# Attention with two value passes, denominators summed by accumulating DMAs, scores two key tiles ahead of the products, and each head's preparation in 28 slots

## The chip, the cores and the metric

The kernel runs on one core of one Trainium2 chip. The metric is the device time of one execution in microseconds (us). The engines of the core are called as the profile calls them: PE (TensorE, the matrix engine; PEld is its weight load), DVE (VectorE), ACT (ScalarE), POOL (GpSimd) and SP (SyncE, which here only issues DMAs). PE multiplies into PSUM, a memory of eight banks of 128 rows by 512 numbers; everything else lies in SBUF or in DRAM.

## The reference

One layer of a hybrid network over 1024 latent tokens and 256 context tokens, with model width 1024. A recurrent branch and an attention branch are gated, added and projected; then a mixture of 16 experts follows. The change touches the attention branch alone, which is

```python
def attend(q_nope, q_rope, k_nope, k_rope, v):
    s = (jnp.einsum('bqhd,bkhd->bhqk', q_nope, k_nope)
         + jnp.einsum('bqhr,bkr->bhqk', q_rope, k_rope)).astype(jnp.float32) * ATTN_SCALE
    prob = jax.nn.softmax(s, axis=-1).astype(v.dtype)
    return jnp.einsum('bhqk,bkhd->bqhd', prob, v)
```

with 8 heads, 1024 queries, 1280 keys (context and latent together), 96 numbers of a query or key (64 and 32) and 64 of a value. Before it the kernel computes the recurrent branch's output projection, after it the attention's output projection, the merge and the experts.

## The kernel before

Matmuls of full precision are split: a float32 array x is kept as a high part xh in the type fp32r and a low part xl = x - xh, made by a cast on ACT and a subtraction on DVE (`split`, lines 94 and 95), and a product takes three fp32r passes, hh, hl and lh (`mm3`, lines 98 to 100). A matmul on plain float32 operands needs no split.

The stage loops over 8 heads (h) and within a head over 10 key tiles (kt) of 128 keys. Keys lie on the partitions and the 1024 queries on the free axis, in two halves (n). For a key tile, `scores` multiplies kh, kl with qh, ql into the PSUM tile s (three buffers), ACT takes the exponential of it into pr, and pr is split into ph and pl. The products then multiply ph, pl with the values into the two PSUM tiles po, one for each half. A value tile vh, vl has 128 columns: 64 are the head's values, the other 64 are ones in vh and zeros in vl, so that 64 rows of po hold the numerators and the other 64 the denominators. Two of the ten tiles (FULL = (0, 5)) go unsplit: pr times a float32 value tile vf. Scores run one key tile ahead of the products.

While a head runs, the next one is prepared (`head_ops`): transposes of its raw keys and queries into the PSUM tiles qkt and their splits kl, ql; 32 matmuls of 320 keys by 128 queries into the PSUM tile pm, each reduced on DVE to its row maximum mx; and two steps `fin` that transpose the maxima (mr) and let ACT write them, negated, into row 0 of qh. All of these share the tag "pm", three PSUM banks. The 40 slots of a head are four for each key tile: before the scores of either half, and before the products of either half. The 39 steps are spread over 34 slots, the second `fin` is in slot 36.

At the head's end `finish` copies numerators (num) and denominators (den) out of po with four ACT copies; po has no second pair of buffers, so the next head's first products wait for them. After each second head `norm_step` takes a reciprocal of den on DVE, multiplies on POOL and splits the result into ath, atl, in eight pieces.

PE's instructions stand in the order in which the code issues them (a manual schedule). On DVE, ACT, POOL and SP a scheduler decides the order when the program is built; it is fixed then, and each engine works through its own order without overtaking. DMAs are issued by SP unless the code says `nc.gpsimd`.

Of the kernel before, what the change touches and what calls it, by code (L numbers as in the profile page):

```python
# [27 lines left out]
P = 128  # L28
# [32 lines left out]
def layer_kernel(ctx: ExitStack, tc: tile.TileContext, I, rope_tab, out, dbg=None):  # L61
# [64 lines left out]
    mod_d = dram.tile([4, D], F32, name="mod_d")  # L126

# [630 lines left out]
    vt = {}  # L758
    for e in range(2):
        for nm, val in (("h", 1.0), ("l", 0.0)):  # L760
            v = p5.tile([P, NKT, P], F32R, name=f"v{nm}{e}")
            vt[nm, e] = v
            o = slice(VH, P) if e == 0 else slice(0, VH)
            nc.vector.tensor_scalar(v[:, :, o], ident[:, None, 0:VH].to_broadcast([P, NKT, VH]), 0.0, val,
                                    op0=OP.mult, op1=OP.add)
    QT, dn, PR = {}, {}, {}
    FULL = (0, 5)
    vf = []
    for e in range(2):
        v = p5.tile([P, len(FULL), P], F32, name=f"vf{e}")  # L770
        nc.gpsimd.memset(v[:, :, slice(VH, P) if e == 0 else slice(0, VH)], 1.0)
        vf.append(v)

# [5 lines left out]
    def load_head(h):  # L779
        kraw = p5.tile([P, 1024], F32, name="kraw", bufs=2)[:, 0:NKT * KA].rearrange("p (t d) -> p t d", d=KA)  # L780
        nc.sync.dma_start(kraw, k_d[h])
        qraw = p5.tile([P, 896], F32, name="qraw", bufs=2)[:, 0:NT * KA].rearrange("p (t d) -> p t d", d=KA)
        nc.sync.dma_start(qraw, q_d[h])
        vraw = p5.tile([P, NKT, VH], F32, name="vraw", bufs=2)
        nc.sync.dma_start(vraw, v_d[h])
        PR[h] = (qraw, kraw, vraw)

    def head_ops(h):
# [6 lines left out]
        mx = p5.tile([P, 64], F32, name="mx", bufs=2)[:, 0:4 * NT].rearrange("p (g t) -> p g t", t=NT)  # L795
        QT[h] = (qh, ql, kh, kl, mx)
        o = slice(0, VH) if e == 0 else slice(VH, P)
# [15 lines left out]
        def pmx(t, g):  # L813
            def f():
                pm = pm1("pm")
                nc.tensor.matmul(pm[:, 0:320], qh[:, t * P:(t + 1) * P], kh[:, g * 320:(g + 1) * 320],  # L816
                                 start=True, stop=True)
                nc.vector.tensor_reduce(mx[:, g, t:t + 1], pm[:, 0:320], axis=AX.X, op=OP.max)  # L818
            return f

        def fin(n):
            def f():
                tt = slice(4 * n, 4 * n + 4)
                nc.vector.tensor_tensor(mx[:, 0:2, tt], mx[:, 0:2, tt], mx[:, 2:4, tt], OP.max)
                nc.vector.tensor_tensor(mx[:, 0, tt], mx[:, 0, tt], mx[:, 1, tt], OP.max)
# [10 lines left out]
        seq += [pmx(t, g) for g in (1, 2, 3) for t in range(4)] + [pmx(t, 0) for t in range(4, 8)]  # L836
        seq += [fin(0)] + [pmx(t, g) for g in (1, 2, 3) for t in range(4, 8)]
# [6 lines left out]
    load_head(1)  # L844
# [13 lines left out]
    for b in range(KD):  # L858
# [11 lines left out]
        for _ in range(len(pre) if b == KD - 1 else max(0, 7 * (b - 1))):  # L870
            if pre:
                pre.pop(0)()
    mrow = p4.tile([16, P], F32, name="mrow2")
# [21 lines left out]
    with pool("p5a") as p5a:  # L895
        def scores(h, kt, side=None):
            qh, ql, kh, kl, _ = QT[h]
            ks = slice(kt * P, (kt + 1) * P)
            pr = p5a.tile([P, SEQ], F32, name="pr", bufs=3)
# [7 lines left out]
            if kt in FULL:  # L907
                return pr, None
            ph = p5a.tile([P, SEQ], F32R, name="ph", bufs=2)
            pl = p5a.tile([P, SEQ], F32R, name="pl", bufs=2)  # L910
            split(ph, pl, pr)
            return ph, pl

        def finish(h, po):
            e, j = h % 2, h // 2
            if e == 0:
                dn["n"] = p5a.tile([P, SEQ], F32, name="num", bufs=1)
                dn["d"] = p5a.tile([P, SEQ], F32, name="den", bufs=1)
            num, den = dn["n"], dn["d"]
# [448 lines left out]
```

## Time and profile before

| | |
|---|---|
| time, median of 3 runs | 1768.45 us (1767.8 to 1769.65) |
| the profiled execution's own time | 1771.81 us |
| its span, first to last instruction | 1769.8 us, so 2.0 us lie around it |
| busy share of the span: PE, PEld, DVE, ACT, POOL | 95%, 77%, 74%, 57%, 15% |
| the attention stage, first scores to last products | from 688.2 to 988.3 us |

Busy time of PE is not PE at its peak: a matmul's record lasts longer than the distance to the next one that follows it without a gap. So the text counts PE's work by the distance between starts. A row of a timeline or of a chain gives the start, the duration, the engine, the line and the operation with its output and inputs; "x2" means that two are merged into the row. A wait row says who waited for whom, the sum, how often, and the longest.

### The profile page before, as it was taken

The numbers are of one execution on the slowest core, as the hardware profiler recorded it, in microseconds if no ns is written. First come the engines' busy times: TensorE is split into PE (matmuls) and PEld (weight loads), VectorE is DVE, ScalarE is ACT, GpSimd is POOL, SyncE is SP. The second block draws the span as 40 slices with busy tenths as digits, with TensorE's granted clock in tenths as the row PEclk, the third lists the DMA queues.
The fourth block names the chain that finished last, engine by engine and source line by source line (L and its number), as shares of the span: only waits on it lengthen the run. The fifth ranks groups of instructions, "written<-read, shape, count | busy, mean of one in ns | idle before, by whom it ended". The sixth has DMA issues, their size and how long they took to land.

```text
span 1769.8 us, 20838 instructions
## 1 busy us (share of the span) xinstructions
PE 1687.1 (95%) x7823; PEld 1356.9 (77%) x7823; DVE 1313.4 (74%) x1607; ACT 1014.9 (57%) x1105; POOL 264.5 (15%) x196
## 2 busy tenths in 40 slices
PE   8999999999999999999999999939999999999996
PEld 3788887888887877777777678827888888888885
DVE  4755456788886454787877657587999999989996
ACT  2533324876788313667776532316777777777773
POOL 1123331211221100111210100020121111112101
PEclk9999999999999999999999999969999999999999
DMA  8264444435443934000000355667999999999981
GB/s 328 100 181 101 108 121 140 131 126 167 155 144 117 318 136 152 28 28 28 29 1 1 138 199 213 234 261 286 379 395 391 403 399 381 399 402 380 389 309 24
DMA packets 174179, 363.72 MB, mean 206 GB/s; under 512 B 40160, under 2 KB 90744, under 8 KB 174080
## 3 DMA queue, kind: packets, MB, share of 16 engines
q1 hardware_dynamic: 168896, 343.54, 53.6%
q0 software_dynamic: 5184, 18.88, 4.0%
q8 instruction: 61, 1.00, 0.2%
q14 instruction: 38, 0.31, 0.0%
HBM read 314.84 MB, written 47.54 MB: 205 GB/s over the span
## 4 chain that ended last, share of the span: by engine, by line
PE 71%; DVE 11%; ACT 6%; issue 4%; DMA 4%; POOL 3%; SPq 0%; POOLq 0%; DVEq 0%; ACTq 0%
PE w_e_gate L99 3%; PE w_e_gate L100 3%; PE w_e_gate L98 3%; PE w_e_down L99 3%; PE w_e_down L100 3%; PE w_e_down L98 3%; PE w_e_up L99 3%; PE w_e_up L98 3%; PE w_e_up L100 3%; PE z L99 2%; PE z L98 2%; PE z L100 2%; PE pm L816 2%; POOL st L143 2%; PE s L98 2%
## 5 line engine op out<-in xcount | busy, mean ns | idle before, releaser
L95 DVE TENSOR_TENSOR el<-ma,eh 128x2048 fp32r<-128x2048 f32 x114 | 258.2, 2286 | 22.2 <-PE w_e_down L99 10.8
L94 ACT CAST eh<-ma 128x2048 fp32r<-128x2048 f32 x114 | 217.9, 1917 | 73.7 <-PE w_e_up L100 28.7
L95 DVE TENSOR_TENSOR el<-me,eh 128x2048 fp32r<-128x2048 f32 x78 | 176.9, 2287 | 16.6 <-ACT eh L94 6.0
L94 ACT CAST eh<-me 128x2048 fp32r<-128x2048 f32 x78 | 149.0, 1916 | 47.4 <-PE w_e_gate L100 17.3
L906 ACT ACTIVATE pr<-s 128x512 f32<-128x512 f32 x160 | 95.8, 599 | 77.2 <-PE s L100 75.8
L818 DVE TENSOR_REDUCE mx<-pm 128x1 f32<-128x320 f32 x256 | 114.4, 483 | 22.8 <-PE pm L816 20.6
L99 PE MATMUL z<-xl,wh 128*128 128x512 f32 x320 | 125.2, 392 | 1.9 <-DVE xl L280 1.9
L98 PE MATMUL z<-xh,wh 128*128 128x512 f32 x320 | 125.2, 393 | 1.0 <-DVE xh L279 0.8
L100 PE MATMUL z<-xh,wl 128*128 128x512 f32 x320 | 125.0, 391 | 1.2 <-POOL wl L326 1.2
L1312 POOL DMA_INDIRECT out_dram<-y,icol x16 | 52.3, 3268 | 469.9 <-DVE y L1311 469.9
L94 ACT CAST wh<-wr 128x1024 fp32r<-128x1024 f32 (+1 forms) x53 | 52.0, 980 | 116.1 <-PE z L99 55.0
L95 DVE TENSOR_TENSOR pl<-pr,ph 128x1024 fp32r<-128x1024 f32 x64 | 81.0, 1265 | 31.4 <-ACT ph L94 24.7
L99 PE MATMUL w_e_up<-el,xgh 128*128 128x512 f32 x256 | 100.7, 394 | 0.6 <-DVE el L95 0.6
L98 PE MATMUL w_e_gate<-eh,xgh 128*128 128x512 f32 x256 | 101.1, 395 | 0.2 <-ACT xgh L94 0.2
L99 PE MATMUL w_e_gate<-el,xgh 128*128 128x512 f32 x256 | 101.2, 395 | 0.0
L100 PE MATMUL w_e_gate<-eh,xgl 128*128 128x512 f32 x256 | 100.1, 391 | 0.8 <-DVE xgl L95 0.8
L98 PE MATMUL w_e_down<-eh,hdh 128*128 128x512 f32 x256 | 99.7, 389 | 1.1 <-ACT hdh L94 1.1
L98 PE MATMUL w_e_up<-eh,xgh 128*128 128x512 f32 x256 | 100.7, 393 | 0.0
L99 PE MATMUL w_e_down<-el,hdh 128*128 128x512 f32 x256 | 100.6, 393 | 0.0
L100 PE MATMUL w_e_down<-eh,hdl 128*128 128x512 f32 x256 | 99.9, 390 | 0.5 <-DVE hdl L95 0.5
L100 PE MATMUL w_e_up<-eh,xgl 128*128 128x512 f32 x256 | 99.8, 390 | 0.0
L816 PE MATMUL pm<-kh,qh 97*128 97x320 f32 x256 | 86.6, 353 | 7.0 <-DVE kl L95 4.1
(349 smaller groups left out, 4368.7 us busy)
## 6 DMA issues: line engine op xcount, KB each, us to landing
ma<-in_w_e_down_dram SPq DMA_DIRECT2D x40, 1024.0 KB, 9.4
ma<-in_w_e_up_dram SPq DMA_DIRECT2D x38, 1024.0 KB, 8.0
ma<-in_w_e_gate_dram SPq DMA_DIRECT2D x36, 1024.0 KB, 7.2
me<-in_w_e_gate_dram SPq DMA_DIRECT2D x28, 1024.0 KB, 7.0
me<-in_w_e_up_dram SPq DMA_DIRECT2D x26, 1024.0 KB, 8.2
me<-in_w_e_down_dram SPq DMA_DIRECT2D x24, 1024.0 KB, 9.8
wr<-in_w_in_dram SPq DMA_DIRECT2D x32, 512.0 KB, 4.5
wr<-in_w_ada_dram SPq DMA_DIRECT2D x32, 512.0 KB, 4.2
```

The source lines that it names most:

```text
L94: nc.scalar.copy(h, src)
L95: nc.vector.tensor_tensor(l, src, h.bitcast(F32), OP.subtract)
L98: nc.tensor.matmul(o, lh, rh, start=start, stop=False)
L99: nc.tensor.matmul(o, lh, rl, start=False, stop=False)
L100: nc.tensor.matmul(o, ll, rh, start=False, stop=stop)
L143: nc.gpsimd.tensor_tensor(ap, ap, h, OP.pow)
L816: nc.tensor.matmul(pm[:, 0:320], qh[:, t * P:(t + 1) * P], kh[:, g * 320:(g + 1) * 320], start=True, stop=True)
L818: nc.vector.tensor_reduce(mx[:, g, t:t + 1], pm[:, 0:320], axis=AX.X, op=OP.max)
L906: nc.scalar.activation(pr[:, sl], sp_, AF.Exp)
L1312: nc.gpsimd.indirect_dma_start(out=out_rows, out_offset=bass.IndirectOffsetOnAxis(ap=icol[:, e:e + 1], axis=0), in_=y, in_offset=None, com ...
```

## The change

Values. A value tile v now holds the high parts in 64 columns and the low parts in the other 64, so a key tile needs two passes, ph and pl, and po holds ph·vh + pl·vh in one half of its rows and ph·vl + pl·vl in the other; `finish` copies one half on ACT and adds the other on DVE. Only one tile is unsplit, FULL = (5,).

Denominators. The ones are gone. The exponentials of key tiles 0 and 1 stay in two tiles "sum"; those of tiles 2 to 9 are added to them by DMAs that POOL issues with an accumulate, even tiles to one, odd to the other, and a last one adds the two. In the next head's key tile 4, `denominators` multiplies the sum with a column of ones (float32, into dp), and four DMAs of SP bring the row through DRAM into 128 partitions for the reciprocal and back, repeated over 64 partitions. The last head sums on PE instead (`last_sums`).

Order. Scores run two key tiles ahead. The row maxima use 24 matmuls, 16 of 512 keys and 8 of 256. The 31 steps of a head's preparation are spread over 28 slots, the second `fin` is in slot 31. kraw, qraw and vraw have one buffer each in place of two, and num takes a buffer of the weight ring "wr".

```diff
-    vt = {}
-    for e in range(2):
-        for nm, val in (("h", 1.0), ("l", 0.0)):
-            v = p5.tile([P, NKT, P], F32R, name=f"v{nm}{e}")
...
+    vt = [p5.tile([P, NKT, P], F32R, name=f"v{e}") for e in range(2)]
-    FULL = (0, 5)
+    FULL = (5,)
...
         def tv():
-            nc.scalar.copy(vt["h", e][:, :, o], vraw)
-            nc.gpsimd.tensor_tensor(vt["l", e][:, :, o], vraw, vt["h", e][:, :, o].bitcast(F32), OP.subtract)
+            nc.scalar.copy(vt[e][:, :, o], vraw)
+            nc.gpsimd.tensor_tensor(vt[e][:, :, o2], vraw, vt[e][:, :, o].bitcast(F32), OP.subtract)
...
-                nc.tensor.matmul(pm[:, 0:320], qh[:, t * P:(t + 1) * P], kh[:, g * 320:(g + 1) * 320],
-                                 start=True, stop=True)
-                nc.vector.tensor_reduce(mx[:, g, t:t + 1], pm[:, 0:320], axis=AX.X, op=OP.max)
+                ks = slice(g * 512, min(TOK, (g + 1) * 512))
+                n = ks.stop - ks.start
+                nc.tensor.matmul(pm[:, 0:n], qh[:, t * P:(t + 1) * P], kh[:, ks], start=True, stop=True)
+                nc.vector.tensor_reduce(mx[:, g, t:t + 1], pm[:, 0:n], axis=AX.X, op=OP.max)
...
-            slots[i * 34 // len(seq)].append(f)
-        slots[36].append(fin(1))
+            slots[i * 28 // len(seq)].append(f)
+        slots[31].append(fin(1))
...
+            if kt < 2:
+                sums[h, kt] = pr
+            elif h < HEADS - 1 or kt < NKT - 2:
+                nc.gpsimd.dma_start(out=sums[h, kt % 2], in_=pr, accum_op=OP.add)
...
-                nc.scalar.copy(den[no, sl], po[n][do, :])
-                nc.scalar.copy(num[no, sl], po[n][no, :])
+                nc.scalar.copy(num[no, sl], po[n][do, :])
+                nc.vector.tensor_tensor(num[no, sl], num[no, sl], po[n][no, :], OP.add)
...
+            if h < HEADS - 1:
+                nc.gpsimd.dma_start(out=sums[h, 0], in_=sums.pop((h, 1)), accum_op=OP.add)
+        def denominators(h, num, rec):
+            acc = sums.pop((h, 0))
+            no = lanes(h)[0]
+            row = rec[no.start:no.start + 1, :]
+            for n in range(2):
+                sl = slice(n * 512, (n + 1) * 512)
+                dp = pm1("dp")
+                nc.tensor.matmul(dp[0:1, :], ones, acc[:, sl], start=True, stop=True)
+                nc.scalar.copy(row[:, sl], dp[0:1, :])
+            nc.sync.dma_start(den_d[h:h + 1, :], row)
+            rs = p5a.tile([P, 8], F32, name="rs", bufs=2)
+            nc.sync.dma_start(rs, den_d[h].rearrange("(p j) -> p j", j=8))
+            nc.vector.reciprocal(rs, rs)
+            nc.sync.dma_start(rec_d[h].rearrange("(p j) -> p j", j=8), rs)
+            row = rec_d[h]
+            nc.sync.dma_start(rec[no, :], bass.AP(tensor=row.tensor, offset=row.offset, ap=[[0, VH], [1, SEQ]]))
...
-                if i + 1 < len(steps):
-                    nxt = scores(*steps[i + 1], side)
+                if i + 2 < len(steps):
+                    ahead2.append(scores(*steps[i + 2], side))
...
+                for t in (ph, pl):
+                    side(2 + (t is pl))
+                    for n in range(2):
+                        sl = slice(n * 512, (n + 1) * 512)
+                        if pl is None and t is ph:
+                            nc.tensor.matmul(po[n], vf[h % 2][:, FULL.index(kt)], ph[:, sl], start=kt == 0, stop=kt == NKT - 1)
+                        elif pl is not None:
+                            nc.tensor.matmul(po[n], vt[h % 2][:, kt], t[:, sl], start=kt == 0 and t is ph,
+                                             stop=kt == NKT - 1 and t is pl)
+                if kt == 4 and h:
+                    denominators(h - 1, dn["n"], dn["r"])
```

Outside this stage the order on every engine is what it was, but for a few loads on SP. On DVE, in a head with no normalisation in it, from the last split of transposed queries (ql) on, before:

```order
L95 TENSOR_TENSOR ql<-qkt,qh 97x512
L818 TENSOR_REDUCE mx<-pm 128x1 x2
L95 TENSOR_TENSOR pl<-pr,ph 128x1024
L818 TENSOR_REDUCE mx<-pm 128x1 x4
L95 TENSOR_TENSOR pl<-pr,ph 128x1024
L818 TENSOR_REDUCE mx<-pm 128x1 x5
```

and now, in the same place:

```order
L95 TENSOR_TENSOR ql<-qkt,qh 97x512
L818 TENSOR_REDUCE mx<-pm 128x1
L95 TENSOR_TENSOR pl<-pr,ph 128x1024
L818 TENSOR_REDUCE mx<-pm 128x1 x3
L95 TENSOR_TENSOR pl<-pr,ph 128x1024
L818 TENSOR_REDUCE mx<-pm 128x1 x6
```

The splits pl now stand between groups of one, three and six reductions, and these reductions are of 512 columns in the first two groups and the first two rows of the third. On ACT, at the end of the third head (h = 2, where the first pair of heads is normalised in the changed kernel), before:

```order
L829 ACTIVATE qh<-mr 1x512
L906 ACTIVATE pr<-s 128x512 x2
L923 COPY den<-po 64x512
L924 COPY num<-po 64x512
L94 CAST kh<-qkt 97x512
L94 CAST qh<-qkt 97x512
```

(the two copies stand there twice, one pair for each half) and now:

```order
L829 ACTIVATE qh<-mr 1x512
L908 ACTIVATE sum<-s 128x512 x2
L94 CAST ph<-sum 128x1024
L94 CAST ath<-num 128x256 x2
L933 COPY num<-po 64x512 x2
L94 CAST kh<-qkt 97x512
L94 CAST qh<-qkt 97x512
```

(exponentials and split of the next head's tiles 0 and 1 stand there twice). Two casts of the normalisation have come ahead of the copies that free po, and these have come behind the split of the next head's tile 1. On POOL, over the same end of a head and into the next one, now:

```order
L916 DMA sum<-pr 128x1024 x2
L941 DMA sum<-sum 128x1024
L969 TENSOR_TENSOR num<-num,rec 128x256 x4
L916 DMA sum<-pr 128x1024
L808 TENSOR_TENSOR v_4669<-vraw,v_4669 128x10x64
L916 DMA sum<-pr 128x1024 x5
```

The products with the reciprocals (L969) stand behind the DMA that adds the two half sums (L941), and that stands behind the last two accumulating DMAs of the head.

## Rows read from the trace of the kernel before

**Rows 1.** By head: length; busy PE, PEld, DVE, ACT, POOL; clock; DMA: heads 1, 2, 7.
```profile
726.70:763.80 37.10, 36.74 (x175) 28.63 (x174) 27.00 (x49) 26.07 (x40) 3.68 (x3) 1.00 0.10 34
763.80:803.90 40.10, 37.91 (x175) 28.16 (x175) 35.02 (x65) 27.68 (x48) 8.80 (x11) 1.00 0.10 31
...
958.30:988.30 30.00, 28.41 (x112) 20.22 (x111) 9.80 (x8) 21.32 (x31) 0.00 (x0) 1.00 0.00 1
sum 300.10, PE 291.12 PEld 221.05 DVE 222.96 ACT 207.62 POOL 38.41; mean PE 36.39 PEld 27.63 DVE 27.87 ACT 25.95 POOL 4.80
```

**Rows 2.** Timeline of PE in the second half of head 1.
```profile
755.23 0.31 PE L816 MATMUL pm<-kh,qh 97*128 97x320 f32 x1
755.37 0.40 PE L98 MATMUL s<-qh,kh 97*128 97x512 f32 x1
755.61 0.40 PE L99 MATMUL s<-ql,kh 97*128 97x512 f32 x1
755.84 0.39 PE L100 MATMUL s<-qh,kl 97*128 97x512 f32 x1
```

**Rows 3.** The chain that ended last, from head 0 into head 1.
```profile
726.66 0.58 ACT den L923
...
729.02 0.49 ACT kh L94
...
729.54 0.70 DVE kl L95
...
730.37 0.39 PE pm L816
730.76 0.86 PE po L963 x2
...
733.55 0.44 PE qkt L803 x4
```

**Rows 4.** Timeline of DVE in head 1.
```profile
754.54 1.21 DVE L95 TENSOR_TENSOR pl<-pr,ph 128x1024 fp32r<-128x1024 f32 x1
755.67 1.28 DVE L818 TENSOR_REDUCE mx<-pm 128x1 f32<-128x320 f32 x3
```

**Rows 5.** Groups by line and shape, 688.2 to 988.3: busy us, mean ns.
```profile
L906 ACT ACTIVATE pr<-s 128x512 f32<-128x512 f32 x160 | 95.8, 599 | 77.2 <-PE s L100 75.8
...
L94 ACT CAST ph<-pr 128x1024 fp32r<-128x1024 f32 x64 | 67.2, 1050 | 1.7
...
L933 DVE RECIPROCAL den<-den 128x128 f32<-128x128 f32 x24 | 21.5, 925 | 5.5 <-ACT den L923 5.5
...
L934 POOL TENSOR_TENSOR num<-num,den 128x128 f32<-128x128 f32 x24 | 17.1, 712 | 110.7 <-DVE den L933 110.7
...
L95 DVE TENSOR_TENSOR kl<-qkt,kh 97x512 fp32r<-97x512 f32 x14 | 9.4, 675 | 15.2 <-ACT kh L94 15.2
...
L95 DVE TENSOR_TENSOR kl<-qkt,kh 97x256 fp32r<-97x256 f32 x7 | 2.9, 411 | 0.0
```

**Rows 6.** Waits of the weight load, 688.2 to 988.3: sum, times, longest.
```profile
PEld pm L816 <- DVE mx L818: 6.8, 13, 1.2
```

**Rows 7.** DMAs that POOL issued, alone in windows of 5.0 (first) and 14.8 us.
```profile
q0 software_dynamic: 144, 0.52, 25.6%
...
s_d<-sg POOLq DMA_DIRECT2D x1, 512.0 KB, 3.1
...
q0 software_dynamic: 144, 0.52, 23.1%
...
out_dram<-y,icol POOLq DMA_INDIRECT x1, 6.1
```

**Rows 8.** The same accumulating scatter over the whole span: median to landing.
```profile
out_dram<-y,icol POOLq DMA_INDIRECT x16, 11.6
```

**Rows 9.** Waits of PE beside the stage: 600 to 690, and 992 to 1060.
```profile
PE qkt L803 <- DVE kl L95: 3.4, 1, 3.4
...
PE mo L98 <- DVE s L1040: 3.1, 1, 3.1
```

More of the change, by code (lines that the diff above doesn't have):

```diff
@@ L770, in layer_kernel @@
         v = p5.tile([P, len(FULL), P], F32, name=f"vf{e}")
-        nc.gpsimd.memset(v[:, :, slice(VH, P) if e == 0 else slice(0, VH)], 1.0)
+        nc.gpsimd.memset(v[:, :, slice(VH, P) if e == 0 else slice(0, VH)], 0.0)
         vf.append(v)
+    onesr = p5.tile([P, P], F32R, name="onesr")
+    nc.vector.tensor_scalar(onesr, ident, 0.0, 1.0, op0=OP.mult, op1=OP.add)
     pmt = ["b"]
@@ L898, in scores @@
             ks = slice(kt * P, (kt + 1) * P)
-            pr = p5a.tile([P, SEQ], F32, name="pr", bufs=3)
+            pr = p5a.tile([P, SEQ], F32, name="sum" if kt < 2 else "pr", bufs=4 if kt < 2 else 3)
             for n in range(2):
@@ L906, in scores @@
                 nc.scalar.activation(pr[:, sl], sp_, AF.Exp)
[L907 to L912, printed above, removed]
-        def finish(h, po):
[L915 to L919, printed above, removed]
-            no, do = (slice(0, VH), slice(VH, P)) if e == 0 else (slice(VH, P), slice(0, VH))
+            if kt not in FULL:
+                ph = p5a.tile([P, SEQ], F32R, name="ph", bufs=3)
+                pl = p5a.tile([P, SEQ], F32R, name="pl", bufs=3)
+                split(ph, pl, pr)
@@ new lines, in scores, with lanes @@
+            if kt < 2:
+                sums[h, kt] = pr
+            elif h < HEADS - 1 or kt < NKT - 2:
+                nc.gpsimd.dma_start(out=sums[h, kt % 2], in_=pr, accum_op=OP.add)
+            return (pr, None) if kt in FULL else (ph, pl)
+        sums = {}
+        def lanes(h):
+            return (slice(0, VH), slice(VH, P)) if h % 2 == 0 else (slice(VH, P), slice(0, VH))
+        def finish(h, po):
+            if h % 2 == 0:
+                dn["n"] = wst.tile([P, SEQ], F32, name="num", tag="wr", bufs=4)
+                dn["r"] = p5a.tile([P, SEQ], F32, name="rec", bufs=1)
+            num = dn["n"]
+            no, do = lanes(h)
@@ new lines, in finish @@
+            if h < HEADS - 1:
[16 more added lines that the diff above has]
+            nc.sync.dma_start(rec[no, :], bass.AP(tensor=row.tensor, offset=row.offset, ap=[[0, VH], [1, SEQ]]))
+            if h % 2:
+                for n in range(4):
+                    norm.append((h // 2, num, rec, slice(n * 256, (n + 1) * 256)))
@@ L940, in layer_kernel @@
         with tc.manual_schedule(engines={mybir.EngineType.PE}):
-            nxt = scores(0, 0)
+            ahead2 = [scores(*steps[j]) for j in range(2)]
             for i, (h, kt) in enumerate(steps):
-                ph, pl = nxt
+                ph, pl = ahead2.pop(0)
                 if kt == 0:
```

67 lines of the change are left out of this document (35 added, 32 removed).

## The prediction
> **What bounds the kernel now.** I read the page first: PE is busy for 95% of the span, so a stage is worth what PE needs in it and what PE waits for. Then I cut the attention stage into its heads [rows 1]. An ordinary head (1) takes 37.1 us; a head at whose start a pair is normalised (2, and 4 and 6 alike) takes 40.1, with DVE 8 us busier; the last one, which prepares nothing, takes 30.0. The stage is 300.1 us. The clock is 1.00 in all of these, so every distance below is one at the full 2.4 GHz. DMA is busy for a tenth of the time.
>
> PE's own work I count by distances between starts. Matmuls of 512 columns follow each other every 0.233 us, one of 320 takes 0.14 [rows 2]. A product on float32 operands takes 0.86, a transpose 0.44/4 = 0.11 [rows 3]. So a head before is 60 score matmuls (13.98), 48 split products (11.18), 4 float32 products (3.44), 32 row maxima (4.48), 18 + 8 transposes (2.86): 35.9 us, or 28.6 without preparation. Eight heads, seven with preparation, make 8 x 28.6 + 7 x 7.34 = 280.2. The other 19.9 us of the stage are waits. An ordinary head has 37.1 - 35.9 = 1.2 of them. Half of that is the chain at the head's end [rows 3]: copies of po from 726.66 on, kh at 729.02, kl at 729.54, and only at 730.37 the first row maximum, which needs the PSUM bank that kl frees. PE issued its last product at 726.9 and had 0.23 for it and 8 + 4 transposes and 6 scores after it, 2.7 us: it stood still for 0.5.
>
> **PE's work after the change.** Products: 36 split matmuls (8.39) and 2 float32 ones (1.72). Row maxima: 16 of 512 columns (3.73) and 8 of 256, which by the slope of [rows 2] take 0.11 (0.88): 4.61, a little more than before. Scores and transposes stay. So 24.1 us without preparation, 7.47 of preparation, and 2 x 0.86 = 1.72 for the denominators of seven heads. The last head's sums on PE are 8 matmuls at 0.233 and 4 at 0.86: 5.3. Sum: 8 x 24.1 + 7 x 7.47 + 7 x 1.72 + 5.3 = 262.4. PE is relieved of **17.8 us**; the third product pass alone gives more, and denominators and last sums take 17.3 back.
>
> **Waits after the change**, which decide. I follow the orders shown above with the durations of the rows; T is the moment at which PE has issued the head's last product.
>
> End of an ordinary head. The scores of the next head's tile 1 now stand just ahead of the four last products, so ACT's second exponential (0.6) and its cast (1.05) [rows 5] last until about T + 0.9, and only then come the two copies, until T + 2. DVE finishes pl of that tile at T + 2.1 (1.13 from start to start [rows 4]), then the two additions (64 rows by 512, read from PSUM, like kl: 0.6 apiece), then kl (0.68 [rows 5]): T + 4.05. PE has 2.7 us of work until the first row maximum. Wait 1.35 where it was 0.5. The casts of kh and qh, the exponentials and vh are queued behind the copies on ACT, but start 0.5 earlier than before.
>
> Row maxima. PE may be three of them ahead of DVE (three banks). A reduction takes (1.28 - 0.48)/2 = 0.40 for 320 columns [rows 4]; kl of 512 and 256 columns differ by 0.264 [rows 5], 1.03 ns a column, so 0.60 for 512 and 0.33 for 256. In key tile 2 stand five of 512: DVE needs 5 x 0.60 + 1.13 = 4.1 us, PE 15 x 0.233 = 3.5. And pl stands ahead of a group of reductions while its cast is not done. Following the order, PE waits 0.5 in tile 2 and 1.0 in tile 3; from tile 4 on, where the denominators give DVE 1.7 us, nothing. I take 1.5 a head; bounds 0 and 3. Before, all waits of this kind were 6.8 us in seven heads [rows 6].
>
> Second `fin`. It moves from the start of tile 9 to the end of tile 7, but its ACT step is behind the cast of tile 9, while PE wants row 0 of the queries for the next head's first scores: 0.35.
>
> So an ordinary head waits 3.2 us where it waited 1.2. The first head has no end before it (2.0), the last no preparation (2.0).
>
> Normalisation. Before, it costs 3.0 us in three heads: DVE takes eight reciprocals of 0.925 [rows 5]. These go to a tile of 8 columns. But now two casts of ath stand ahead of the copies on ACT, wait for POOL's products, and these stand behind the DMA that adds the half sums. The last accumulate of the head can start some 5.5 us before T, lands (5.2, below) at T - 0.3, and two products of 256 columns (between 0.71 and 1.42 each [rows 5]) take until T + 2, the two casts behind them until some T + 2.4. The copies so start 1.5 us later than T + 0.9; I put all of that on PE, at the ends of heads 2, 4 and 6.
>
> Waits: 2.0 + 6 x 3.2 + 2.0 + 3 x 1.5 = 27.7 instead of 19.9, **7.8 more**.
>
> **What lies beside.** Each head has eight accumulating DMAs of 512 KB and one that adds the halves. The trace has no such DMA within SBUF. A plain one that POOL issued landed in 3.1 us, an accumulating scatter with a quiet DMA system in 6.1 [rows 7], among the experts' weights in 11.6 [rows 8]. The queue's share tells the packet: 25.6% x 16 engines x 5.0 us / 144 = 0.142 us plain, 23.1% x 16 x 14.8 / 144 = 0.380 accumulating. Nine packets an engine make 1.3 and 3.4; so 3.1 + 2.1 = 5.2 us, near the quiet scatter; bounds 3.1 and 11.6. Adds to one tile wait for each other, four to a half sum, and POOL's queue keeps both halves in step: a head needs 4 x 5.2 + 2 issues, some 22 us of 36. Hidden behind PE, at no cost. The Trainium skill (DMA: Bandwidth & Descriptors, "Anatomy of one DMA") gives 2.0 us plus bytes at 436 GB/s, which would be 3.2 us a link by my estimate; with that the normalised ends would wait up to 2 us less and the sum would be 4 to 6 us lower; the packets of these rows are 2.7 times as long when they accumulate, so I don't take it. The four DMAs of SP for a denominator, about 3 us each, run from tile 4 to the head's end, 14 us; if they are late, POOL's products are, and by ACT the next head's po.
>
> Before the stage, one buffer for vraw makes SP wait with the third head's vraw until POOL has used the second's; the store and load of sg are queued behind it, and PE waits there now for kl behind sg, 3.4 us [rows 9]. With 1.2 MB less loaded ahead of it I take 0, bounds -3.4 and +4. After the stage three reciprocals run ahead of the last copies, and the first 27 matmuls mo need no ath of the last pair (6.3 us of cover); PE's 3.1 us wait for DVE there [rows 9] stays: 0, bounds -2 and +2. The experts' stage is PE's and only moves.
>
> **The sum:** -17.8 + 7.8 = -10.0 us, on the profiled execution 1771.81 to 1761.8. That stands 3.4 us above the median; from the median, 1768.45 - 10 = **1758.4 us** (0.57% faster). About 0.2% (3.5 us) is what a measurement of this kernel can tell from no change.
>
> **Rivals.** (1) The second look-ahead swallows the waits: a head waits 1.2 as now and normalisation is free. 262.4 + 8 x 1.2 = 272, so 1740. For it: the products of a tile have two tiles of slack. Against: the waits come from po and the pm banks, which no look-ahead of scores touches. (2) DVE becomes the bound in the packed part: bank waits of 3 instead of 1.5, 7 heads, +10.5: 1769, no change. For it: DVE's demand in tiles 0 to 2 is above PE's. Against: over a head DVE has about 27.5 us of work in 36, and order decides where it is. (3) The accumulating chain binds: slower. Head time is then 4 links and two issues; it decides from about 8.5 us a link. With the 11.6 of [rows 8], 4 x 11.6 + 1 = 47.4 us, 10 more than 37.5, in seven heads: +70 - 10, 1828. For it: that row is the commonest accumulate in the trace. Against: there the DMA engines were full, here a tenth. The Trainium skill (the same page, "Rules for kernel authors") says that an add must wait for the semaphore of the one before it on the same bytes, which is what makes this a chain; no run here shows its length. (4) SP's queue, late weights: +4 to +10 on a forecast that lost its gain, 1772.
>
> **Chances.** Forecast 0.50 (own range 1748 to 1766), (1) 0.20, (2) 0.15, (3) 0.10, (4) 0.05. Faster 0.69, same 0.16, slower 0.15. The range leaves out (3) and little else: 1738 to 1773.
>
> **What would show it.** Right: ordinary heads of about 36.5 us, those after heads 2 and 4 about 38, the last about 32; pm waiting for kl at head starts and for mx in tiles 2 and 3; accumulates landing in 5 to 6 us; stage about 290. Wrong: links above 8 us with POOL in step with the heads; dp waiting for a DMA; PE idle in tiles 4 to 9; a longer wait at qkt before the stage.

## The result and the profile after

The changed kernel takes 1792.78 us (median of 4, 1790.72 to 1793.96), the kernel before in runs beside it 1768.12 (1766.53 to 1769.65): the ratio is 1.0125 [1.0109, 1.0141], **1.25% slower** (1.0125 is the ratio on record, as are those below; the two medians alone would give 1.0139). The prediction said 1758.4 in a range of 1738 to 1773; it was wrong in size and in sign. One of the four runs of experiment 5 took 7504 us, at a mean granted clock of 0.21, and is left out of its ratio.

The profiled execution took 1793.96 us, with a span of 1792.2, 22.4 us more than before. I cut both spans at the starts of the same instructions: up to the first score +1.1, the attention stage +13.5 (314.5 instead of 301.0; [rows 1] has 300.1 for it because its first window begins at 688.2, and the first score starts at 687.53), the merge and projection behind it +2.9, the router -0.4, the experts +2.5, and from PE's last matmul to the end +2.7. So most of it is in the stage that was to gain 10. Its heads, by windows that end with a head's last product (the columns are those of [rows 1]), heads 0 (its window begins behind the scores of tiles 0 and 1), 1, 3, 5 and 7:

```profile
692.80:727.50 34.70, 32.82 (x152) 24.72 (x151) 28.00 (x43) 25.27 (x38) 8.01 (x10) 1.00 0.79 177
727.50:765.40 37.90, 34.78 (x155) 24.85 (x154) 29.30 (x46) 26.98 (x42) 10.04 (x11) 1.00 0.78 165
...
803.40:846.40 43.00, 36.63 (x156) 26.52 (x155) 32.88 (x50) 28.59 (x46) 13.15 (x15) 0.92 0.67 145
...
884.40:927.80 43.40, 36.82 (x155) 26.75 (x154) 32.90 (x50) 28.50 (x46) 13.15 (x15) 0.92 0.67 144
...
966.00:1003.50 37.50, 31.81 (x110) 21.90 (x109) 17.25 (x19) 22.27 (x34) 8.80 (x11) 0.86 0.70 161
```

Heads 2, 4 and 6 are like head 1, 38.0. PE's busy time fell in an ordinary head, as the sum had it (34.8 where [rows 1] has 36.7 for head 1), yet the heads became longer. Heads 3 and 5, at whose start a pair is normalised, take 5.0 to 5.5 us more than their neighbours, and their mean granted clock is 0.92, the last head's 0.86, where it was 1.00 in the heads of [rows 1]. The waits of PE in the stage (sum, times, longest):

```profile
PE pm L817 <- DVE kl L95: 16.1, 9, 5.2
PE pm L817 <- DVE mx L818: 8.1, 14, 0.8
PE po L1016 <- DVE num L934: 5.7, 1, 5.7
PE s L98 <- ACT qh L829: 1.4, 7, 0.2
```

The dearest is the first row maximum's wait for kl, forecast at 1.35 each; the longest of them is 5.2. One such place, the start of head 3, on four engines. PE's timeline first:

```profile
806.09 0.40 PE L100 MATMUL s<-qh,kl 97*128 97x512 f32 x1
811.46 0.76 PE L817 MATMUL pm<-kh,qh 97*128 97x512 f32 x1 [4.98 <-DVE kl L95]
...
815.86 0.61 PE L802 MATMUL qkt<-ident,qraw 128*97 128x128 f32 x4
```

DVE's timeline at the same time:

```profile
804.59 4.26 DVE L95 TENSOR_TENSOR pl<-sum,ph 128x1024 fp32r<-128x1024 f32 x1 [1.07 <-ACT ph L94]
808.78 0.74 DVE L95 TENSOR_TENSOR atl<-num,ath 128x256 fp32r<-128x256 f32 x2
809.45 1.27 DVE L934 TENSOR_TENSOR num<-num,po 64x512 f32<-64x512 f32 x2
810.64 0.67 DVE L95 TENSOR_TENSOR kl<-qkt,kh 97x512 fp32r<-97x512 f32 x1
```

POOL's timeline:

```profile
798.26 0.84 POOL L916 DMA_DIRECT2D sum<-pr  x1 [1.78 <-ACT pr L908]
804.11 0.85 POOL L941 DMA_DIRECT2D sum<-sum  x1 [5.01 <-DMA sum<-pr]
804.67 3.09 POOL L969 TENSOR_TENSOR num<-num,rec 128x256 f32<-128x256 f32 x4
```

ACT's timeline, where the copies free po:

```profile
806.44 0.40 ACT L94 CAST ath<-num 128x256 fp32r<-128x256 f32 x1 [0.28 <-POOL num L969]
806.87 1.07 ACT L933 COPY num<-po 64x512 f32<-64x512 f32 x2
```

The last of the four DMAs on SP's queue that bring the reciprocals:

```profile
797.79 0.46 SPq L959 DMA_DIRECT2D rec<-rec_d  x1
```

Read them from the last one up. The reciprocals are asked for at 797.79 and land 5.0 us later, about 802.8. POOL has stood since 799.1 at L941, which waits until the head's last accumulate has landed; its products, whose operands have been there since 802.8, start at 804.67, all four at once. Just then DVE starts the subtraction pl of the next head's tile 1. It takes 1.2 us elsewhere [rows 4] and here 4.26: it ends 1.1 us after POOL's products do. The subtractions atl, the additions that free po, and kl stand behind it on DVE, and PE stands still for 5 us, 3.5 more than at an ordinary head's start (1.5). Then the clock, in slices of 2 us:

```profile
804.00:806.00 2.00, 2.00 (x15) 1.80 (x14) 1.41 (x1) 0.80 (x2) 1.89 (x3) 1.00 0.33 66
...
808.00:810.00 2.00, 0.00 (x0) 0.00 (x0) 2.00 (x4) 2.00 (x5) 0.00 (x0) 0.76 0.01 0
810.00:812.00 2.00, 0.54 (x1) 0.50 (x2) 2.00 (x5) 1.74 (x4) 0.87 (x1) 0.50 0.00 0
812.00:814.00 2.00, 2.00 (x7) 1.64 (x6) 2.00 (x3) 0.46 (x2) 0.00 (x0) 0.50 0.98 197
814.00:816.00 2.00, 2.00 (x7) 1.47 (x7) 1.52 (x4) 0.84 (x2) 1.32 (x1) 0.53 0.97 254
816.00:818.00 2.00, 2.00 (x13) 1.70 (x12) 0.79 (x2) 1.84 (x4) 0.33 (x1) 1.00 0.39 114
```

While PE stands still the granted clock falls to 0.50, which is 1.2 GHz, and it is 1.00 (2.4 GHz) again in the slice from 816 on, with PE at work since 811.46. From there to 815.86 PE did nine matmuls of 512 columns and two transposes, 2.3 us by [rows 2, 3]; they took 4.4. So a normalised head's start costs 3.5 us of wait and 2.1 of clock more than an ordinary one's: 5.6, and the windows show 5.0 and 5.5.

The two engines meet in the ordinary heads too. In head 2, POOL's timeline at the subtraction that makes the next head's low values:

```profile
771.10 1.88 POOL L808 TENSOR_TENSOR v<-vraw,v 128x640 fp32r<-128x640 f32 x1
```

and DVE's at the next pl:

```profile
771.85 2.23 DVE L95 TENSOR_TENSOR pl<-pr,ph 128x1024 fp32r<-128x1024 f32 x1
```

Here too pl ends 1.1 us after POOL's instruction. This was so already in the kernel before, in its head 2. POOL's timeline there:

```profile
769.45 1.57 POOL L809 TENSOR_TENSOR vl<-vraw,vh 128x640 fp32r<-128x640 f32 x1 [1.92 <-ACT vh L808]
```

and DVE's:

```profile
770.35 1.74 DVE L95 TENSOR_TENSOR pl<-pr,ph 128x1024 fp32r<-128x1024 f32 x1
```

So the trace of before showed the meeting, in the longest pl and not in the one of [rows 4]. What it costs an ordinary head is small. PE's timeline in head 2 of the changed kernel:

```profile
768.13 0.40 PE L100 MATMUL s<-qh,kl 97*128 97x512 f32 x1
770.05 0.47 PE L817 MATMUL pm<-kh,qh 97*128 97x512 f32 x1 [1.53 <-DVE kl L95]
...
773.57 0.63 PE L1016 MATMUL po<-ph,v 128*128 128x512 f32 x2
774.47 0.50 PE L817 MATMUL pm<-kh,qh 97*128 97x512 f32 x1 [0.27 <-DVE kl L95]
...
777.99 0.50 PE L817 MATMUL pm<-kh,qh 97*128 97x512 f32 x1 [0.50 <-DVE mx L818]
...
781.12 0.39 PE L817 MATMUL pm<-kh,qh 97*128 97x256 f32 x1 [0.64 <-DVE mx L818]
```

By the distances between starts PE lost 1.7 us at the first maximum (768.13 to 770.05, less 0.23), 0.4 at the one whose kl stands behind the held pl (773.57 to 774.47, less 2 x 0.23), 1.45 at the two that wait for a bank (0.65 and 0.8) and 0.35 at the second `fin`: 3.9 in all. The head takes 38.0, and its own work is 33.3 by the prediction's count; the remaining 0.8 is in steps of about 0.1, most of them behind a transpose or a wait, which stand in no wait row.

The accumulates themselves do what was forecast (DMAs of the stage, median to landing):

```profile
sum<-pr POOLq DMA_DIRECT2D x62, 512.0 KB, 4.7
sum<-sum POOLq DMA_DIRECT2D x7, 512.0 KB, 4.4
```

Behind the stage two things differ. Between the last gate and the last product of the experts there is a short gap in both kernels (1.3 and 1.1 us of waits), and in this execution of the changed one the clock falls at it:

```profile
1763.00:1765.00 2.00, 0.97 (x8) 0.73 (x8) 2.00 (x1) 1.49 (x2) 0.00 (x0) 0.94 0.00 0
1765.00:1767.00 2.00, 1.90 (x4) 1.08 (x5) 1.24 (x2) 0.02 (x1) 0.00 (x0) 0.50 0.00 0
```

That is 2.4 us, and the 2.4 in the merge are of the same kind; both come and go with the execution: the kernel before has the first of them in experiment 17, and the stretch of the merge that takes 13.5 here takes 11.0 in experiments 1, 2 and 5, whose code is the same there. The other is the end. The last matmul and the last DMA issue of the changed kernel:

```profile
1779.10 0.39 PE L100 MATMUL w_e_down<-eh,hdl 128*128 128x512 f32 x1
...
1781.08 1.55 POOL L1364 DMA_INDIRECT out_dram<-y,icol  x1 [26.41 <-DVE y L1363]
```

and those of the kernel before:

```profile
1759.39 0.39 PE L100 MATMUL w_e_down<-eh,hdl 128*128 128x512 f32 x1
...
1761.38 1.55 POOL L1312 DMA_INDIRECT out_dram<-y,icol  x1 [23.95 <-DVE y L1311]
```

From the end of the issue to the end of the span are 9.6 us (1792.2 - 1782.63) where there were 6.9 (1769.8 - 1762.93).

### The profile page after: what moved, and what is told of

Its sections match the earlier page's. It is cut to its first block, busy times and chain, and to the rows that moved or that the text cites. A ratio compares the mean times of both kernels' runs of the same rounds, so it can differ in the third digit from the quotient of the medians.

```text
span 1792.2 us, 20689 instructions
## 1 busy us (share of the span) xinstructions
PE 1679.5 (94%) x7675; PEld 1341.7 (75%) x7675; DVE 1320.7 (74%) x1535; ACT 1019.4 (57%) x1099; POOL 306.5 (17%) x245
## 5 line engine op out<-in xcount | busy, mean ns | idle before, releaser
L818 DVE TENSOR_REDUCE mx<-pm 128x1 f32<-128x512 f32 (+1 forms) x192 | 108.2, 594 | 18.0 <-PE pm L817 17.3
L908 ACT ACTIVATE pr<-s 128x512 f32<-128x512 f32 x128 | 76.8, 601 | 68.7 <-PE s L100 53.3
L95 DVE TENSOR_TENSOR pl<-pr,ph 128x1024 fp32r<-128x1024 f32 x56 | 72.5, 1294 | 34.9 <-ACT ph L94 30.9
L817 PE MATMUL pm<-kh,qh 97*128 97x512 f32 (+1 forms) x192 | 73.0, 399 | 25.6 <-DVE kl L95 16.1
```

Of the source, the lines that this page charges most:

```text
L95: nc.vector.tensor_tensor(l, src, h.bitcast(F32), OP.subtract)
L817: nc.tensor.matmul(pm[:, 0:n], qh[:, t * P:(t + 1) * P], kh[:, ks], start=True, stop=True)
L818: nc.vector.tensor_reduce(mx[:, g, t:t + 1], pm[:, 0:n], axis=AX.X, op=OP.max)
L908: nc.scalar.activation(pr[:, sl], sp_, AF.Exp)
```

## The experiments

Each changes the changed kernel by the lines shown, unless it says otherwise; the ratio is to the kernel before, on the same chip. Every edit lets the scheduler order DVE, ACT, POOL and SP anew, so other instructions can move with it. Heads are told by the distance between last products, "stage" from the first score to the last product (301.0 before, 314.5 changed). Theory **A** says that the casts of ath hold po's copies on ACT (the prediction's working). Theory **B** says that POOL's products, all at once and late, hold DVE's pl. For what makes them late, **Q** is POOL's queue, where they stand behind L941, and **D** is the DMA traffic, under which rec lands in 5.0 us.

**1. The second half of the normalisation after tile 3, so that nothing of it is ahead of the copies.**

```diff
-                if norm and (kt < 4 or kt > 7):
+                if norm and kt < 4:
```

> The four normalisation steps of a pair all stand in key tiles 0 to 3 of the next head (norm and kt < 4), so no cast of ath stands ahead of the copies of po on ACT. POOL's order stays: its four products still run right behind the DMA that adds the half sums. Theory A (the casts, which wait for POOL, hold up the copies): heads 3 and 5 fall from 43 to some 38.5 us and head 7 from 37.4 to 32, 1778 us. Theory B (the long thing is the subtraction pl on DVE, 4.3 us in place of 1.2 while POOL's products run): pl stays at 4.3, kl comes only 1 us earlier, the clock still falls; 1789 us.

1797.76 us (1790.68 to 1802.93), 1.0170 [1.0147, 1.0192]. The casts are gone from ahead of the copies, and at the start of head 3 the wait stays, 4.3 us. DVE's timeline there:

```profile
806.20 4.26 DVE L95 TENSOR_TENSOR pl<-sum,ph 128x1024 fp32r<-128x1024 f32 x1 [1.08 <-ACT ph L94]
```

and POOL's:

```profile
806.26 3.10 POOL L969 TENSOR_TENSOR num<-num,rec 128x256 f32<-128x256 f32 x4
```

At the start of head 5, in the same execution, pl begins 0.39 us ahead of POOL's products and is not held. DVE's timeline:

```profile
890.13 1.23 DVE L95 TENSOR_TENSOR pl<-sum,ph 128x1024 fp32r<-128x1024 f32 x1 [1.08 <-ACT ph L94]
```

and POOL's:

```profile
890.52 3.51 POOL L969 TENSOR_TENSOR num<-num,rec 128x256 f32<-128x256 f32 x4
```

There PE waits 1.3 us for the first maximum. Head 3 takes 45.9 us and head 5 40.5; in both PE waits a further 2.2 for the second maxima (mr). The scheduler gives POOL the four products at once wherever the code has them. A falls as the main cause, B stands.

**2. The same with the products on DVE** (`nc.vector` in L969 besides the line above).

> As e1_norm_late, and the products num times rec run on DVE in place of POOL. Theory B (POOL's products keep DVE out of the subtraction pl): pl stays at 1.2 us at the ends of heads 2, 4 and 6, the clock stays at 1.00, heads 3 and 5 take some 39.5 us (3.3 us more work on DVE in them costs one or two), head 7 some 32.5: 1781 us. Theory C (what counts is that the reciprocals land late, whoever multiplies): DVE waits for them in its own order, heads 3 and 5 stay at 42 or more: 1790 us.

1789.46 us (1787.03 to 1793.84), 1.0111 [1.0088, 1.0135]. At the start of head 3 PE now waits 1.6 and the clock stays at 1.00, and pl takes 1.2 there with all the accumulating DMAs in place: so POOL's products held it, not the DMA traffic. But B's 1781 us are missed: heads 3 and 5 still take 42.2 and 41.5, because the second maxima (mr) come late in tiles 4 and 5 and the clock falls there. The wait moved on; of the stage's length 4.4 us were gained (310.1).

**3. No accumulates in heads 0 to 6.** Left out is the summation: denominators come from tile 0 alone, and rs gets 1 added.

```diff
-            elif h < HEADS - 1 or kt < NKT - 2:
+            elif h == HEADS - 1 and kt < NKT - 2:
...
-                nc.gpsimd.dma_start(out=sums[h, 0], in_=sums.pop((h, 1)), accum_op=OP.add)
+                sums.pop((h, 1))
```

> The accumulating DMAs of heads 0 to 6 and the adds of half sums are left out (69 fewer DMAs issued by POOL); the denominators of these heads so hold key tile 0 alone, plus one. Theory: the 2.7 us by which the end of the kernel is longer than before (from the last product of the experts to the last instruction, 13.1 for 10.4) come from POOL's last drain, which grows with the DMAs that POOL issued: 10.4 again. POOL's products no longer stand behind the landing of an accumulate and start 1.5 us earlier: heads 3 and 5 fall by 1 to 2, ordinary heads stay at 37.9: 1787 us. Rival (the accumulating traffic itself slows the engines' work in SBUF): ordinary heads fall by 1 us or more: 1775 us.

1777.66 us (1772.9 to 1778.82), 1.0030 [1.0010, 1.0050]; stage 299.0. rec lands in 3.3 us, heads 3 and 5 take 37.9 and 37.8, and the end from the last matmul is 10.7 instead of 13.1. "Hidden, at no cost" was wrong: without the accumulates the stage is 15.5 us shorter and the end 2.4, and the ratio falls by 0.95%, 17 us. All ordinary heads still take 37.5 to 37.6, where 36.5 was forecast. The pl beside POOL's subtraction for v takes 1.76 in head 2, and the wait behind it, 0.4 in the changed kernel, is gone.

**4. Only L941 left out** (the last two lines of the diff above; the denominators then hold the even tiles alone, and rs gets 1 added as there).

> Only the DMA that adds the odd half sum to the even one is left out (7 DMAs; the denominators of heads 0 to 6 so hold the even key tiles alone, plus one); the 56 accumulates stay. The orders of ACT and DVE around the head's end are those of e8_no_acc, so the two differ by the accumulates alone. Theory Q (the products stand in POOL's queue behind that DMA, which waits for the landing of the last accumulate, and then meet the last subtraction pl): heads 3 and 5 at 38 to 39 us, head 7 at 34, no half clock at the heads' ends: 1779 us. Theory D (the accumulates' traffic itself makes the reciprocals land late and holds the engines): heads 3 and 5 stay at 42 or more: 1790 us.

1783.83 us (1781.99 to 1788.71), 1.0089 [1.0066, 1.0111]; stage 307.0, heads 3 and 5 40.2 and 40.1. POOL is free early, and now waits for rec, which lands in 4.6. Its timeline:

```profile
805.04 4.16 POOL L970 TENSOR_TENSOR num<-num,rec 128x256 f32<-128x256 f32 x4 [2.90 <-DMA rec<-rec_d]
```

and DVE's:

```profile
805.32 1.54 DVE L95 TENSOR_TENSOR pl<-sum,ph 128x1024 fp32r<-128x1024 f32 x1 [1.99 <-ACT ph L94]
```

From 43.2 to 40.2 is Q's, 3 us a head; the 2.3 from there to the 37.9 of experiment 3 are D's. They come by the prediction's own chain, A: counted from T, the start of the head's last product (806.4), the copies begin at T + 2.4 and kl ends at T + 5.7, where the prediction's terms give T + 2.4 and T + 5.55. This time POOL's products take longer (4.16) and pl hardly (1.54): where the two meet, one or the other waits.

**5. Denominators earlier** (`kt == 4` becomes `kt == 2`).

> The denominators' column products and their four DMAs start behind key tile 2 in place of 4, so the reciprocals land some 7 us earlier and POOL multiplies in key tiles 7 and 8, ahead of the last accumulates. Theory A and B alike (the stop at the ends of heads 2, 4 and 6 comes from products that are late): heads 3 and 5 fall to 38.5, head 7 to 32, the clock stays at 1.00 there: 1778 us. Rival (the column products meet the landing of the last DMA in tile 2 and PE waits there instead, or more work in the packed tiles costs the same): 1790 us or more.

1792.8 us, 1.0126 [1.0105, 1.0147]. The reciprocals then wait in the middle of the head, the casts of ath that stand there on ACT wait for them, and PE waits up to 4.7 for the second maxima behind those casts. The starts of heads 3 and 5 are cured (both take 37.9), but heads 2 and 4 now take 45.4 and 43.6 and head 6 40.0. The wait has moved ahead; no gain.

**6. The preparation spread over 31 slots** (`i * 28` becomes `i * 31`).

> The 31 steps of a head's preparation in slots 0 to 30 in place of 0 to 27, the widest that scores two tiles ahead allow. If the packing makes the waits of an ordinary head (4.6 us, of which about 2 are waits of the row maxima for a bank that DVE has not freed), an ordinary head falls from 37.95 to about 36.8: 7 heads, 1785 us. If the waits come from the head's start (copies of po, casts, kl), they stay: 1793 us.

1793.71 us (1790.22 to 1799.51), 1.0144 [1.0115, 1.0172]. The waits for mx shrink to 2.7 and kl's to 1.0, but 11.5 us of mr and 4.7 of qh come up, since the last steps of the preparation are now too near to the next head's scores, which run two tiles ahead. The total stays.

**7. One tile of look-ahead, and with it 34 slots as before.**

```diff
-            slots[i * 28 // len(seq)].append(f)
-        slots[31].append(fin(1))
+            slots[i * 34 // len(seq)].append(f)
+        slots[36].append(fin(1))
...
-            ahead2 = [scores(*steps[j]) for j in range(2)]
+            ahead2 = [scores(*steps[j]) for j in range(1)]
...
-                if i + 2 < len(steps):
-                    ahead2.append(scores(*steps[i + 2], side))
+                if i + 1 < len(steps):
+                    ahead2.append(scores(*steps[i + 1], side))
```

> The order of before with the new arithmetic: scores one key tile ahead, 34 slots, second fin in slot 36. If look-ahead and packing cost time by themselves (the first row maximum of a head waits 1.5 us and more because the exponential and cast of a second tile stand ahead of the copies), ordinary heads fall from 37.95 to about 36.5 and the whole to 1782 us. If the second tile of look-ahead is what hides the casts and subtractions, heads grow by 1 us or more: 1800 us.

1783.1 us (1782.13 to 1784.17), 1.0079 [1.0062, 1.0096]; stage 302.6. Heads 1, 5 and 6 take 36.7 to 36.9; heads 2 and 4, in which POOL's products now stand, 39.1.

**8. One tile of look-ahead with the 28 slots kept** (the last two pieces of that diff).

> Scores one key tile ahead, but the preparation still in 28 slots and the second fin in slot 31: one half of what e6_ahead1 undoes. If the second tile of look-ahead is what costs an ordinary head its 1.2 us: ordinary heads at 36.7 as in e6_ahead1, 1783 us. If it is the packing: 37.9 as after the change, 1792 us.

1794.24 us (1792.52 to 1794.43), 1.0140 [1.0123, 1.0157]; ordinary heads 38.5. So the gain of experiment 7 is neither the look-ahead's nor (experiment 6) that of more slots alone: a longer preparation pays only with the shorter look-ahead, which lets it end later.

**9. Experiments 7 and 3 together** (the summation left out as in 3).

> e6_ahead1 with the accumulates and adds of half sums left out as in e8_no_acc. If the two costs are separate, they add: heads with preparation at some 36.4 us, the stage at 291, the end at 10.7: 1768 us, no faster than before in spite of 17.8 us less on PE. If they are one cost seen twice: 1776 us.

1772.93 us (1771.18 to 1780.93), 1.0025 [1.0009, 1.0041]; stage 294.9, 19.6 less than the changed kernel's. The two alone gave 11.9 and 15.5, so they overlap by 7.8: in part they are cures for the same waits.

**10. and 11. POOL's order written by hand too** (`engines={PE, Pool}` in the manual schedule, with the line of experiment 1), with two tiles of look-ahead and with one (and the 34 slots of experiment 7).

> As e1_norm_late, and POOL's order is that of the code, so that its four products run one in each of key tiles 0 to 3 and not all at once at the head's end. Theory B: no pl longer than 2.1 us, no stop at the ends of heads 2, 4 and 6, clock 1.00, heads 3 and 5 at some 38.8 us, head 7 at 32: 1779 us. Theory C: casts of ath and what stands behind them wait in tiles 0 to 3 instead, 41 us or more: 1788 us.

> e6_ahead1 (scores one tile ahead, 34 slots, second fin in slot 36) with the normalisation of e9_pool_order. If both findings add: all heads with preparation at some 36.8 us, head 7 at 33, 1775 us; still above 1768 because the new arithmetic's 17.8 us less on PE stand against waits of 3.5 us a head, and the end is 2.7 longer. If the slack of the second tile of look-ahead is needed once DVE has the products' splits in the packed tiles: 1783 us as e6_ahead1 or more.

1803.97 us, 1.0182 [1.0152, 1.0212], and 1796.82, 1.0143 [1.0112, 1.0174]. Both miss. In code order POOL meets waits of its own, and DVE's reductions and splits come late behind them: 16.8 us of waits for mx in the first, 11.0 for ql in the second.

**12. Experiment 7 with the unsplit tile 0 given back** (`FULL = (0, 5)`).

> e6_ahead1 with two unsplit key tiles again, FULL = (0, 5). PE gets 0.8 us more a head (two float32 products of 0.86 for four of 0.233), DVE and ACT lose a subtraction and a cast just where the head starts. If PE's waits there are for that work (1.5 us a head and more), 1779 us; if not, 6 us more than e6_ahead1: 1789 us.

1780.79 us (1775.58 to 1784.24), 1.0070 [1.0049, 1.0092]; stage 295.8. POOL's products and pl meet here too. POOL's timeline:

```profile
797.55 3.11 POOL L969 TENSOR_TENSOR num<-num,rec 128x256 f32<-128x256 f32 x4
```

and DVE's:

```profile
797.80 3.95 DVE L95 TENSOR_TENSOR pl<-pr,ph 128x1024 fp32r<-128x1024 f32 x1 [1.27 <-ACT ph L94]
```

**13. The same with the product on DVE:**

```diff
-            nc.gpsimd.tensor_tensor(num[:, sl], num[:, sl], rec[:, sl], OP.mult)
+            nc.vector.tensor_tensor(num[:, sl], num[:, sl], rec[:, sl], OP.mult)
```

> e17_ahead1_full2 with the products num times rec on DVE in place of POOL. In e17 the subtraction pl of key tile 9 takes 3.95 us while POOL's four products run, and PE waits 2.08 for it at the ends of heads 2, 4 and 6. If it is the meeting of the two engines, pl is 1.2 again, the wait goes and heads 2, 4 and 6 fall from 38.0 to some 36.5: 1776 us. If the reciprocals land late, DVE waits for them with pl behind it: 1781 us or more.

1769.09 us (1767.39 to 1772.89, 12 runs) against 1775.98 (1769.22 to 1780.87) of the kernel before beside it: 0.9971 [0.9959, 0.9983], **faster than the kernel before by 0.3%**, with experiment 14 the only version below 1. Beside the other experiments the kernel before took 1768 to 1772 us, so what shows the gain is the stage more than the whole. Its heads 1 and 3, by windows as above (head 2 takes 36.0):

```profile
730.70:766.30 35.60, 35.22 (x155) 24.79 (x154) 27.08 (x44) 26.07 (x41) 10.64 (x12) 1.00 0.79 173
...
802.30:837.90 35.60, 35.28 (x155) 24.86 (x154) 27.71 (x47) 26.37 (x42) 10.66 (x12) 1.00 0.80 174
```

and the dearest wait of PE in the stage:

```profile
PE pm L817 <- DVE mx L818: 1.6, 7, 0.3
```

The stage takes 285.2, 15.8 less than before. The span gained only 4.2 of them: the stage begins 6.3 us later, the merge is 2.3 longer, and the end takes 3.0 more.

**14. The same with two buffers for vraw** (`ph` and `pl` cut from three to two to make room), to see whether the late start is vraw's.

> e18_full2_dve with two buffers for vraw (room for it comes from two buffers of ph and pl in place of three, which scores one tile ahead need no more). If one buffer of vraw makes the wait at qkt ahead of the stage longer (5.1 us and more in place of 3.4, since the store and load of sg stand behind vraw's load in SP's queue), that wait is 3.4 again: 2 us less than e18. If not, the same time as e18.

1772.18 us (1767.11 to 1776.02), 0.9980 [0.9966, 0.9993]; the wait at qkt is 6.8 us and the stage starts at 694.0. It isn't vraw's buffer.

**15. Experiment 13 without the second unsplit tile** (`FULL = (5,)`).

> e18_full2_dve with one unsplit key tile in place of two. If the cast and subtraction of key tile 0 cost PE more at a head's start than the 0.8 us of its float32 products, heads take 36.7 where e18 takes 35.6: 1778 us. Otherwise 6 us less than e18: 1764 us.

1777.07 us (1772.69 to 1780.22), 1.0029 [1.0019, 1.0039]; stage 295.1. So the unsplit tile 0 is worth 9.9 us in the stage (and 10 by the two ratios), though it costs PE 0.8 a head more (2 x 0.86 for 4 x 0.233, by [rows 2, 3]): it spares ACT and DVE a split just where they are late. Beside experiment 7 (302.6), the product on DVE gives 7.5.

**16. The changed kernel's order with the unsplit tile 0 and the product on DVE.**

> The changed kernel with two unsplit key tiles, FULL = (0, 5), and the products on DVE, but its order kept: scores two tiles ahead, preparation in 28 slots. Against e18_full2_dve it differs by look-ahead and packing alone. If these cost as between e6 and the change, ordinary heads take 37 us or more where e18 takes 35.6, 1.4 x 7 = 10 us: 1781 us. If the collision of POOL and DVE was the whole trouble: 1771 us.

1834.86 us, 1.0350 [1.0333, 1.0368]. The dearest wait of PE in the stage:

```profile
PE po L1014 <- DMA sum<-pr: 44.4, 8, 9.7
```

The unsplit product of tile 0 reads the sum tile; with two tiles of look-ahead it stands in the code behind the accumulate of tile 2 into that tile, so it waits until this has landed (and multiplies tile 0 plus tile 2: the output is another). The time can't tell what was asked. It shows why the look-ahead of two and the second unsplit tile exclude each other.

**17. The kernel before once more.**

> The kernel before, once more with a profile, to see on the same chip how far its first stages and its end vary from one execution to the next. If the first scores start at 687 to 689 us again and the end (from the last product) takes 10.4, the 693.9 of e18_full2_dve and its 13.4 are that kernel's own; if they start at 692 or later, they are the execution's.

1769.84 us (1765.95 to 1776.18), 0.9992 [0.9979, 1.0004]. Its end takes 10.35 us again, where versions with accumulates have 12.9 to 13.6; so that is the versions' own. Its last up to last down products take 17.1, where its first profile has 15.5: the clock in the tail is the execution's.

## Why the prediction was wrong

**PE's work: right**, as far as the runs show it. PE is busy for 1.9 us less in an ordinary head, where the forecast work is 2.6 less; and experiment 13, which by the sum has 6 us more work for PE than the change, runs the stage in 285.2.

**Waits: wrong, and that is all of it.** 27.7 us were forecast, 52.1 came (314.5 - 262.4, the lower clock included). 0.9 of the difference is the stretch of the stage that [rows 1] leaves out; the forecast stage, 301.0 - 10 = 291.0, was missed by 23.5:
- *"I put all of that on PE, at the ends of heads 2, 4 and 6"*: 1.5 us each were forecast for the normalisation. Heads 3 and 5 took 43.2 where 38 was said, 10.5 together, and the last head began with a wait of 5.7. The step that failed is the overlap: it counted POOL's products by their own duration (right, 0.77 each) and let DVE's pl go on beside them. At the start of head 3 pl took 3.1 us more, and kl ends at T + 7.9 (T is 803.4) where T + 5.55 follows from the prediction. The other part is the queue: POOL gets past the wait at L941 at T + 0.7, where T - 0.3 was forecast, and so the copies begin 1.1 later than forecast. rec was in time for that, and would bind next (experiment 4). Experiments 1 (head 3 beside head 5), 2, 12 and 13 show DVE's subtraction held; 3 and 4 show the two causes of the lateness. The clock's 2.1 us stood in no term.
- *"Hidden behind PE, at no cost"*: the accumulates cost 15.5 us in the stage and 2.4 behind it (experiment 3). Their length was right, 4.7 for 5.2, and the chain doesn't bind, so rival 3 falls. What they cost is others' time: POOL's queue behind them, rec's slower landing, and the end.
- *Ordinary heads*: 38.0 for 36.5, four heads, 5.8 us. The wait of 3.2 took the place of all of the 1.2 before, of which the prediction had explained 0.5; the other 0.7 it put at nothing without a reason, and 0.8 of that kind are there again. The head's start cost 1.7 for 1.35, and the pl held by POOL's subtraction for v, 2.23 for 1.2, cost 0.4 that was in no term (experiment 3 without it: 37.5). The bank waits (1.45 for 1.5) and fin's (0.35) were right, so rival 2 falls.
- The first and the last head together take 76.2 us from the first score on, 7.2 longer than the sum had them (291.0 - 4 x 36.5 - 2 x 38). By the terms of the sum the first should take 33.6 and the last 34.6 (24.1 + 1.72 + 5.3 + 2.0 + 1.5; the 32 among the signs does not fit the sum). The last took 37.4, with a wait of 5.7 at its start and a clock of 0.86. The first took 38.85, 0.9 of which is the stretch said above; its first 4.2 us ran at a mean clock of 0.62, and the stage of the kernel before begins at the lower clock too (0.50 from 689.5 to 691.5). What else holds the first head is not worked out.

**Outside the stage** 0 was forecast, and 8.8 came, all but 0.2 of it in three places: 2.7 at the end, which is the kernel's own; 4.8 in merge and experts, which come and go with the clock; 1.1 ahead of the stage, where PE's wait at qkt grew from 3.4 [rows 9] to 5.1 and is 1.7 in experiment 17. What delays it is open: vraw's buffer isn't it (experiment 14). Rival 4 had the place, and a small part of the loss.

Rival 1 was no rival to the mechanism as put, since the second look-ahead swallows nothing (experiment 8 does without it in the same time). Its stage of 272 is in no run; the nearest is 285.2, by the opposite edit (experiment 13).

The Trainium skill (SBUF — State Buffer, "Who interferes with whom") states that a VectorE operation with two inputs in SBUF and a GpSimd operation that reads SBUF exclude each other, for a whole instruction. Of the rules that speak against this change it is the one that I did not weigh. The rows agree that one of them waits: in the five places shown where pl is held, that of the kernel before among them, it ends 1.1 us behind the end of POOL's instructions. They add that four products in a row can act as one: pl was held through all four, 3.1 us, though by the record it had started 0.08 us ahead of the first (POOL's spans are rough). It need not be so: in experiment 4 pl starts 0.28 us behind POOL's first product and takes 1.54, in experiment 12 0.25 behind it and takes 3.95. What decides between the two is open.

## What to carry to other kernels

Before work is put on POOL or behind a DMA that POOL issues, list what stands behind that DMA in POOL's queue and which two-input operation of DVE runs when the queue is released; price the meeting at the sum of both. The longest instance of an instruction in the trace of before, not its usual one, shows whether two engines hold each other (pl, 1.74 beside 1.21). A gap of 5 us on PE cost two more in clock, so a late product isn't worth its own lateness only. A longer look-ahead takes away the room in which the preparation may end: here one tile with 34 slots, one more unsplit tile and the product on DVE brought the stage 15.8 us below the kernel before, while the change as made, two tiles ahead with 28 slots, stands 13.5 above it.

## What the runs showed of the hardware

- DVE's subtraction of 128 by 1024 from SBUF takes 1.2 us. Beside four of POOL's products, 3.09 us by themselves, it took 3.95 to 4.26 in three of the places shown; in two others POOL's stretched instead, to 4.16 and 3.51, and DVE's took 1.54 and 1.23.
- From the last DMA that POOL issues to the end of the kernel it takes 2.7 us longer with 69 more DMAs issued by POOL in the program; with 63 of them left out (experiment 3) all but 0.3 of it is gone.
- The same short gaps left the clock at 2.4 GHz in one execution of a kernel and let it fall to 1.2 in another (15.5 and 17.1 us for the same work of the kernel before).
- rec, 256 KB from DRAM on SP's queue, lands in 3.3 us without the accumulates, in 4.6 with those of a head but not L941, and in 5.0 with all, which keep the DMA engines busy for 0.67 to 0.79 of a head.
